# First tiles and PSUM banks of the SwiGLU and of the last part laid over other memory, and the first SwiGLU products in another order

## The chip, the cores and the metric

The program runs on one core of one Trainium2 chip. The metric is the device time of one execution in microseconds (us), as a median of several runs. PE is TensorE, DVE VectorE, ACT ScalarE, POOL GpSimd, and SP SyncE, which issues every DMA of this kernel. A named tile such as `wg` lies in SBUF or in PSUM; a name that ends in `_d` is a tensor in DRAM.

## The reference

One layer of a backbone with 2048 latent tokens of width 1024: gated linear attention (GLA, in both directions, with 256 context tokens ahead), its out projection, a residual, and a SwiGLU network of hidden width 2816 with another residual. Everything is float32.

```
h_lat = modulate(rms_norm(x, norm_g[0]), mod[0], mod[1])
o     = head_rms_norm(o_forward + flip(o_backward), gla_norm_g)
y_lat = (o * silu(r)) @ gla_w_out                          # out projection
lat   = x + mod[2] * rms_norm(y_lat, norm_g[1])
h     = modulate(rms_norm(lat, norm_g[2]), mod[3], mod[4])
gate, up = split(h @ ffn_w_in)                             # SwiGLU, first layer
out   = lat + mod[5] * rms_norm((silu(gate) * up) @ ffn_w_out, norm_g[3])
```

## The kernel before

Each float32 product is three matmuls on high and low parts. A matrix that comes from DRAM in float32 is therefore first cast to a rounded high part on ACT, and the low part, source minus high part, is formed on DVE.

The program has four stages, each with its own pools of tiles, taken as stacks on the left and the right side of SBUF and PSUM. A pool may lie over an earlier pool's memory, and its first write then waits for that memory's last readers.

- **Prologue, projections, attention**, up to about 828 us. The two scan states `Tf` and `Tb` come from the context tokens.
- **Out projection** (`p2`), 828 to 1078 us: for each block `gc` of 128 rows from 15 down to 0, steps `b0` (loads; the backward state `E` from `Tb` or from the block before), `b1` (products `o<-E,qb`, L695), `b2` (norm, transposes `tp` L722, gate), `b3` (products `py`, L86 to L88) and `b4` (norm, residual, store of `l1`, L754). After each four blocks `h2_units` makes transposed SwiGLU input: `first` (L769) writes two block matrices to `T_d`; `second` loads them back (`bl`, L775 and L776), and forms the sums and differences of Strassen's method (L781) and stores them (L778, L782).
- **SwiGLU, first layer** (`p3`), 1078.7 to 1944.6 us: 88 features of 7 products each, with the weight block as the stationary operand (`whl`, cast at L933, low part L934) and one of 7 tiles `T` as the moving one (L951). A product is 12 matmuls, 128x512. `load_T` (L860 to L862) loads a `T` tile in four DMAs of 256 KB, each with a cast and a subtraction. The order of products in the chain is P1, P2, P6, P7, P5, P4, P3; X collects P1, P6, P5 and P3, Y is P2, and Z collects P7 and P4. Row half 1 is worked first, then half 0; the `T` tiles of half 0 are loaded over those of half 1 as these fall free.
- **Last part** (`p4`), 1955 to 2383 us: products of the SwiGLU sums `ar` (loaded from `S_d`, `ring`, L1023 to L1028) with blocks of the second weight matrix `wr` (from `wraw`, `w2_block`, L1036 to L1038) in PSUM banks X and W (L1074), then norm, residual and the result.

A scheduler decides the order in which instructions stand in each engine's queue; the engines then work their queues in order. SP issues all DMAs in its order, so a DMA whose semaphore isn't there yet holds up all behind it. In addition each DMA shares one of eight semaphores with the DMA eight places ahead, and waits for that one.

At the end of the out projection, 4 units of `second` for half 1 of the SwiGLU input are still to be made (`pend`); the loads of the `T` tiles for P7, P5, P4 and P3 go into a pool `hR` on the right side, which opens only when these units' tiles are closed.

Of the kernel before, what the change touches and what calls it, by code (L numbers as in the profile page):

```python
# [34 lines left out]
def trunk(ctx, tc, x, cx, modw, cols, rows, consts, wqkr, wv, wvg, wgate, wout, w1, w2, out):  # L35
# [17 lines left out]
    qb_d = [dram.tile([128, H, 128], F32, name=f"qb_d{c}") for c in range(NC_)]  # L53

# [120 lines left out]
    Tf = gp.tile([128, H, DV], F32, name="Tf")  # L175
    glt = [c1.tile([128, 128], F32R, name=f"glt{i}") for i in range(4)]
# [177 lines left out]
    def gla_stages(g, i, c, first):  # L354
# [279 lines left out]
    p2t = ExitStack()  # L634
    sp = p2.enter_context(tc.tile_pool(name="sp", bufs=2, reuse_waits="tile"))
# [14 lines left out]
    def back(gc):  # L650
# [13 lines left out]
        def b0():  # L664
# [3 lines left out]
            qb = sp.tile([128, H, 128], F32, name="qb2", tag="qb2", bufs=3)  # L668
# [124 lines left out]

    order = list(range(NC_ - 1, -1, -1))
# [28 lines left out]
    for i, gc in enumerate(order):  # L823
# [27 lines left out]
    hR = p3.enter_context(tc.tile_pool(name="hR", bufs=1, reuse_waits="tile", side="right"))  # L851
    ps3z = p3.enter_context(tc.tile_pool(name="ps3z", bufs=1, space=PSUM, reuse_waits="tile", side="right"))
    T = {}

    def load_T(p, i):
        pool = hL if i in (P1, P2, P6) else hR
        t = pool.tile([128, 4, 2, GT], F32R, name=f"T{i}", tag=f"T{i}", bufs=1)
        for k in range(4):
            raw = t[:, k, 1, :].bitcast(F32)
            sync.dma_start(out=raw, in_=T_d[p][i][k])  # L860
            nc.scalar.copy(out=t[:, k, 0, :], in_=raw)  # L861
            nc.vector.tensor_sub(out=t[:, k, 1, :], in0=raw, in1=t[:, k, 0, :].bitcast(F32))  # L862
        T[i] = t
# [130 lines left out]
    feats = {}  # L994
    for i in CHAIN:
        load_T(1, i)
    n = len(seq)
    for t in range(n + 1):
        if t < n:
            feats[t] = Feat(*seq[t])  # L1000
        for lag, i in ((0, P1), (1, P5), (0, P2), (1, P4), (0, P6), (1, P3), (0, P7)):
            j = t - lag
            if not 0 <= j < n:
# [6 lines left out]
        if t >= 2 and t % 2 == 0:  # L1010
# [12 lines left out]
    def ring(tag, src):  # L1023
        t = r4.tile([128, 2, 512], F32R, name=tag, tag=tag, bufs=14)
# [6 lines left out]
    def w2_block(i, fp):  # L1031
# [158 lines left out]
```

## Time and profile before

| | |
|---|---|
| three runs | 2386.19, 2387.81, 2392.54 us, median 2387.81 |
| the profiled execution | 2384.77 us, of it a span of 2383.0 us in the trace |
| PE busy | 2302.0 us, 97% of the span |
| DVE, ACT, POOL busy | 1557.7, 1068.8 and 186.6 us |
| mean granted clock of PE | 0.986 of full speed |
| DMA | 463.98 MB, mean 195 GB/s |

All times below are microseconds from the start of the span. A queue name with q, such as SPq, stands for the sequencer of an engine. "[7.09 <-ACT whl L933]" behind a row says that the engine was idle for 7.09 us before it, and that the last event that it waited for was the ACT instruction of L933 that writes `whl`. PE matmuls overlap, so their durations sum to more than the time between their starts.

### The profile page before, as it was taken

How to read it: one execution, taken by the hardware profiler on the slowest of the kernel's cores; microseconds unless marked ns; L12 is line 12 of the kernel's file. 1: busy time of each engine (PE TensorE's matmuls, PEld its weight loads, DVE VectorE, ACT ScalarE, POOL GpSimd, SP SyncE). 2: the span in 40 equal slices, each digit the busy share in tenths (PEclk: the TensorE clock that was granted, in tenths of full speed). 3: DMA queues.
4: the chain of work that ended last, by engine and by line, in shares of the span. 5: the costliest groups of instructions: out<-in, count | busy, mean ns of one | idle time of the engine just before them, and what ended most of it. 6: DMA issues, size and time to landing. Idle time of an engine off the chain costs nothing.

```text
span 2383.0 us, 32426 instructions
## 1 busy us (share of the span) xinstructions
PE 2302.0 (97%) x11546; PEld 1939.9 (81%) x11546; DVE 1557.7 (65%) x2478; ACT 1068.8 (45%) x1947; POOL 186.6 (8%) x274
## 2 busy tenths in 40 slices
PE   8999999999998999897999999999999989999998
PEld 4898898898898878685888888888888868888887
DVE  6756666766658576658776666866666647466554
ACT  3535445445547544335433333533333336554552
POOL 1100000000001033631000000000000000001001
PEclk9999999999999999997999999999999999999999
DMA  8765468565455587758787332633233248559655
GB/s 299 225 208 173 148 197 285 177 210 208 153 191 191 206 274 257 243 186 309 258 264 259 125 111 93 230 102 115 97 106 107 75 149 284 191 192 330 201 181 177
DMA packets 228902, 463.98 MB, mean 195 GB/s; under 512 B 22530, under 2 KB 66178, under 8 KB 228740
## 3 DMA queue, kind: packets, MB, share of 16 engines
q1 hardware_dynamic: 228740, 461.92, 57.3%
q8 instruction: 90, 1.47, 0.3%
q14 instruction: 72, 0.59, 0.1%
HBM read 331.27 MB, written 130.56 MB: 194 GB/s over the span
## 4 chain that ended last, share of the span: by engine, by line
PE 52%; DMA 0%; DVE 0%; SPq 0%; ACT 0%; issue 0%; POOLq 0%; POOL 0%; ACTq 0%
PE X L951 20%; PE Z L951 10%; PE X L1074 10%; PE W L1074 8%; PE Y L951 5%; DMA wraw<-w 0%; DMA T<-T_d 0%; DMA T_d<-hf 0%; DVE sa L984 0%; DVE bl L781 0%; DVE y L1055 0%; SPq L906 0%; DVE t L781 0%; DVE hf L781 0%; DVE a L974 0%
## 5 line engine op out<-in xcount | busy, mean ns | idle before, releaser
L951 PE MATMUL X<-T,whl 128*128 128x512 f32 x2112 | 495.7, 390 | 8.2 <-ACT whl L933 7.1
L951 PEld LDWEIGHTS X<-T,whl 128*128 128x128 f32 x2112 | 396.6, 188 | 91.5 <-ACT whl L933 7.5
L951 PE MATMUL Z<-T,whl 128*128 128x512 f32 x1056 | 256.2, 391 | 9.1 <-ACT T L861 9.1
L1074 PE MATMUL X<-wr,ar 128*128 128x512 f32 x1056 | 242.3, 391 | 10.6 <-ACT wr L1038 10.6
L1074 PEld LDWEIGHTS X<-wr,ar 128*128 128x128 f32 x1056 | 199.2, 189 | 52.8 <-ACT wr L1038 11.1
L951 PEld LDWEIGHTS Z<-T,whl 128*128 128x128 f32 x1056 | 199.3, 189 | 51.6 <-ACT T L861 9.5
L86 PE MATMUL pj<-hhi,whi 128*128 128x512 f32 (+1 forms) x544 | 213.6, 395 | 2.1 <-DVE hhi L75 1.4
L87 PE MATMUL pj<-hlo,whi 128*128 128x512 f32 (+1 forms) x544 | 211.4, 389 | 0.0
L88 PE MATMUL pj<-hhi,wlo 128*128 128x512 f32 (+1 forms) x544 | 210.4, 387 | 0.0
L73 ACT CAST whi<-wf 128x1024 fp32r<-128x1024 f32 x104 | 109.0, 1048 | 192.7 <-PE pj L87 84.4
L1028 DVE TENSOR_TENSOR ar<-ar 128x512 fp32r<-128x512 f32 x154 | 106.2, 691 | 131.1 <-ACT ar L1027 130.6
L76 DVE TENSOR_TENSOR wlo<-wf,whi 128x1024 fp32r<-128x1024 f32 x104 | 126.8, 1220 | 86.5 <-ACT whi L73 81.0
L1074 PE MATMUL W<-wr,ar 128*128 128x512 f32 x792 | 180.5, 389 | 0.0
L1074 PEld LDWEIGHTS W<-wr,ar 128*128 128x128 f32 x792 | 148.7, 188 | 30.8
L1027 ACT CAST ar<-ar 128x512 fp32r<-128x512 f32 x154 | 95.5, 621 | 154.6 <-DMA ar<-S_d 107.0
L86 PE MATMUL pj<-whi,hhi 128*128 128x256 f32 x432 | 125.0, 289 | 6.3 <-DVE gs L292 4.9
L951 PE MATMUL Y<-T,whl 128*128 128x512 f32 x528 | 127.7, 390 | 0.0
L87 PE MATMUL pj<-wlo,hhi 128*128 128x256 f32 x432 | 123.2, 285 | 2.8 <-DVE wlo L76 2.8
L88 PE MATMUL pj<-whi,hlo 128*128 128x256 f32 x432 | 122.7, 284 | 0.0
L87 PEld LDWEIGHTS pj<-hlo,whi 128*128 128x128 f32 x544 | 103.5, 190 | 21.3 <-DVE hlo L76 2.2
L86 PEld LDWEIGHTS pj<-hhi,whi 128*128 128x128 f32 x544 | 103.1, 191 | 21.5 <-DVE hhi L75 1.6
L88 PEld LDWEIGHTS pj<-hhi,wlo 128*128 128x128 f32 x544 | 103.4, 190 | 19.7
(231 smaller groups left out, 4273.7 us busy)
## 6 DMA issues: line engine op xcount, KB each, us to landing
ar<-S_d SPq DMA_DIRECT2D x154, 256.0 KB, 3.0
wf<-wqkr SPq DMA_DIRECT2D x68, 512.0 KB, 3.9
wg<-w SPq DMA_DIRECT2D x44, 512.0 KB, 3.5
wu<-w SPq DMA_DIRECT2D x88, 256.0 KB, 2.7
S_d<-sa SPq DMA_DIRECT2D x88, 256.0 KB, 2.0
wr<-W_d SPq DMA_DIRECT2D x88, 256.0 KB, 3.0
wf<-wv SPq DMA_DIRECT2D x36, 512.0 KB, 3.8
wl<-w SPq DMA_DIRECT2D x66, 256.0 KB, 3.7
```

The lines of the kernel that those rows point to most:

```text
L73: nc.scalar.copy(out=hi, in_=src)
L76: nc.vector.tensor_sub(out=lo, in0=src, in1=hi.bitcast(F32))
L86: nc.tensor.matmul(out=ps, lhsT=ahi, rhs=bhi, start=start, stop=False)
L87: nc.tensor.matmul(out=ps, lhsT=ahi, rhs=blo, start=False, stop=False)
L88: nc.tensor.matmul(out=ps, lhsT=alo, rhs=bhi, start=False, stop=stop)
L951: nc.tensor.matmul(out=ps, lhsT=w[:, a, ks], rhs=t[:, k, b, :], start=first and k == 0 and n == 0, stop=k == 3 and n == 2, skip_group_chec ...
L1027: nc.scalar.copy(out=t[:, 0, :], in_=raw)
L1028: nc.vector.tensor_sub(out=t[:, 1, :], in0=raw, in1=t[:, 0, :].bitcast(F32))
L1074: nc.tensor.matmul(out=po[j], lhsT=a[:, x, 128 * j:128 * j + 128], rhs=w[:, z, :], start=first and fp == 0 and n == 0, stop=fp == NFP - 1 ...
```

## The change

In the attention part the state `Tb` loses its own pool, lies in that stage's pool, and is stored in DRAM (`Tb_d`, 512 KB); the out projection loads it back into a `ub2` buffer. The buffers of `qb2` go from 3 to 2. A new pool `hG` at the bottom of the out projection's left side holds the `T` tile of P1, which is loaded inside the out projection (`gc == 3`). The SwiGLU's weight pool `w3` comes ahead of `hL`, `hL` takes P2, P6 and P7, and `hR` P5, P4 and P3. The first products of two features are written out by hand. In the last part the ring of 14 `ar` and 14 `wr` tiles is cut into a first share (4 `ar` in `rA`, 10 `wr` and the 4 `wraw` in `rB`) and a rest (`rC`), and the X banks move to the right side of PSUM.

```diff
@@ attention part @@
-    tbp = pT.enter_context(tc.tile_pool(name="tbp", bufs=1))
-    Tb = tbp.tile([128, H, DV], F32, name="Tb")
+    Tb = gp.tile([128, H, DV], F32, name="Tb")
...
+                        st.dma_start(out=Tb_d, in_=Tb.rearrange("p h v -> p (h v)"))
@@ out projection @@
+    hG = p3.enter_context(tc.tile_pool(name="hG", bufs=1, reuse_waits="tile"))
-            qb = sp.tile([128, H, 128], F32, name="qb2", tag="qb2", bufs=3)
+            qb = sp.tile([128, H, 128], F32, name="qb2", tag="qb2", bufs=2)
             if gc == NC_ - 1:
+                Tb = sp.tile([128, H, DV], F32, name="ub2", tag="ub2", bufs=2)
+                sync.dma_start(out=Tb.rearrange("p h v -> p (h v)"), in_=Tb_d)
...
+        if gc == 3:
+            load_T(1, P1)
     p2.close()
@@ SwiGLU @@
+    w3 = p3.enter_context(tc.tile_pool(name="w3", bufs=2, reuse_waits="tile"))
     hL = p3.enter_context(tc.tile_pool(name="hL", bufs=1, reuse_waits="tile"))
-    w3 = p3.enter_context(tc.tile_pool(name="w3", bufs=2, reuse_waits="tile"))
...
-    for u in pend:
-        u()
-    p2t.close()
-    hR = ...
-        pool = hL if i in (P1, P2, P6) else hR
+    T_pool.update({i: hL for i in (P2, P6, P7)})
...
-    for i in CHAIN:
-        load_T(1, i)
+    feats = {0: Feat(*seq[0]), 1: Feat(*seq[1])}
+    load_T(1, P2)
+    for j, i in ((0, P1), (1, P1), (0, P2)):
+        feats[j].product(i)
+    load_T(1, P6)
+    feats[1].product(P2)
+    load_T(1, P7)
+    pend.pop(0)()
+    feats[0].product(P6)
+    for u in pend:
+        u()
+    p2t.close()
+    hR = p3.enter_context(tc.tile_pool(name="hR", bufs=1, reuse_waits="tile", side="right"))
+    ps3z = p3.enter_context(tc.tile_pool(name="ps3z", bufs=1, space=PSUM, reuse_waits="tile", side="right"))
+    T_pool.update({i: hR for i in (P3, P4, P5)})
+    for i in (P5, P4, P3):
         load_T(1, i)
+    for j, i in ((0, P7), (1, P6), (1, P7), (0, P5), (0, P4), (0, P3)):
+        feats[j].product(i)
-    for t in range(n + 1):
+    for t in range(2, n + 1):
@@ last part @@
-    r4 = p4.enter_context(tc.tile_pool(name="r4", bufs=1, reuse_waits="tile"))
+    rA = p4.enter_context(tc.tile_pool(name="rA", bufs=1, reuse_waits="tile"))
     y4 = p4.enter_context(tc.tile_pool(name="y4", bufs=1, reuse_waits="tile"))
+    rB = p4.enter_context(tc.tile_pool(name="rB", bufs=1, reuse_waits="tile"))
+    rC = p4.enter_context(tc.tile_pool(name="rC", bufs=1, reuse_waits="tile"))
...
+    def slot(tag):
+        i = count[tag] % 14
+        count[tag] += 1
+        first, nf = {"ar": (rA, 4), "wr": (rB, 10)}[tag]
+        pool, sfx, nb = (first, "", nf) if i < nf else (rC, "2", 14 - nf)
+        return pool.tile([128, 2, 512], F32R, name=tag, tag=tag + sfx, bufs=nb)
...
-        raw = r4.tile([128, 512], F32, name="wraw", tag="wraw", bufs=4)
+        raw = rB.tile([128, 512], F32, name="wraw", tag="wraw", bufs=4)
```

Four places show how the queues move. A row is the line of code, the operation, what it writes and reads, and the shape; line numbers behind the change are those of the changed code, a few higher or lower than before.

The first is SP's queue where the out projection starts (`ub2`, `qb2` and `op2` are the loads of `b0`, `wof` the weights of the out projection). Before:

```order
L667 DMA ub2_8324<-ub_d15_160 128x1024
L669 DMA qb2_8326<-qb_d15_176 128x512
L671 DMA op2_8328<-op_d15_144 128x1024
L645 DMA wof_8348<-wout 128x1024
L645 DMA wof_8352<-wout 128x1024
L659 DMA rt_8364<-r_d3_77 128x4x128
L246 DMA r_d3_77<-stg_8398 128x512
L667 DMA ub2_8423<-ub_d14_159 128x1024
L645 DMA wof_8356<-wout 128x1024
L645 DMA wof_8360<-wout 128x1024
```

And after:

```order
L669 DMA ub2_8326<-ub_d15_160 128x1024
L671 DMA qb2_8328<-qb_d15_176 128x512
L673 DMA op2_8330<-op_d15_144 128x1024
L679 DMA ub2_8332<-Tb_d_177 128x1024
L647 DMA wof_8352<-wout 128x1024
L647 DMA wof_8356<-wout 128x1024
L661 DMA rt_8368<-r_d3_77 128x4x128
L245 DMA r_d3_77<-stg_8402 128x512
L669 DMA ub2_8427<-ub_d14_159 128x1024
L647 DMA wof_8360<-wout 128x1024
L647 DMA wof_8364<-wout 128x1024
```

The load of `Tb` stands behind block 15's three loads, ahead of the weights; the load of block 14's `ub2` now takes the buffer that the state lay in, and so waits for the ACT operation that forms block 15's `E`. On PE the first `o` products of block 15 stand 17 matmuls (`pj`) further back in the queue than before.

The second is SP's queue at the end of the out projection (`l1_d1` and `l1_d0` are the last residual stores, `T0`, `T1`, `T5`, `T6`, `T4` the tiles of P1, P2, P6, P7 and P5, `wg` and `wu` the first weights of the SwiGLU, `bl` the loads of a unit of `second`). Before:

```order
L860 DMA T5_10965<-T_d15_90 128x512 x3
L754 DMA l1_d1_114<-y2_10622 128x1024
L775 DMA bl_10823<-T_d00_78 128x512
L776 DMA bl_10823<-T_d01_79 128x512
L860 DMA T5_10965<-T_d15_90 128x512
L903 DMA wg_11030<-w1 128x1024
L906 DMA wu0_11032<-w1 128x512
L906 DMA wu1_11033<-w1 128x512
L870 DMA wl_11113<-w2 128x512
L754 DMA l1_d0_113<-y2_10732 128x1024
L775 DMA bl_10850<-T_d00_78 128x512
L776 DMA bl_10850<-T_d01_79 128x512
```

And after, first the weights:

```order
L758 DMA l1_d1_114<-y2_10639 128x1024
L903 DMA wg_10839<-w1 128x1024
L906 DMA wu0_10841<-w1 128x512
L906 DMA wu1_10842<-w1 128x512
L903 DMA wg_10845<-w1 128x1024
L906 DMA wu0_10847<-w1 128x512
L906 DMA wu1_10848<-w1 128x512
L804 DMA T1_10851<-T_d11_86 128x512
```

then what follows them:

```order
L758 DMA l1_d0_113<-y2_10749 128x1024
L804 DMA T1_10851<-T_d11_86 128x512 x3
L804 DMA T5_10918<-T_d15_90 128x512 x4
L804 DMA T6_10949<-T_d16_91 128x512 x4
L779 DMA bl_10962<-T_d00_78 128x512
L780 DMA bl_10962<-T_d01_79 128x512
L782 DMA T_d02_80<-hf2_10972 128x512
L779 DMA bl_11012<-T_d00_78 128x512
L780 DMA bl_11012<-T_d01_79 128x512
```

The weights of two features now come straight behind the store `l1_d1` and ahead of all other `T` tiles, and the `bl` loads of the first unit, which stood right behind `l1_d1` before, come behind eleven `T` loads that follow `l1_d0`.

The third is PE's queue at the same place, from the last product of the out projection on (X, Y and Z are the PSUM tiles; the numbers of the `T` tiles, before: 10939 P1, 10952 P2, 10965 P6, 10978 P7, 10991 P5; after: 10485 P1, 10851 P2, 10918 P6, 10949 P7, 11101 P5). Before:

```order
L951 MATMUL X<-T_10939,whl 128x512 x3
L951 MATMUL Y<-T_10952,whl 128x512 x4
L102 MATMUL tp<-ident,xh 128x128 x4
L951 MATMUL Y<-T_10952,whl 128x512 x6
L951 MATMUL X<-T_10965,whl 128x512 x12
L951 MATMUL X<-T_10939,whl 128x512 x12
L951 MATMUL Y<-T_10952,whl 128x512 x12
L951 MATMUL Z<-T_10978,whl 128x512 x12
L951 MATMUL X<-T_10991,whl 128x512 x12
```

And after:

```order
L951 MATMUL X<-T_10918,whl 128x512 x3
L100 MATMUL tp<-ident,xh 128x128 x5
L951 MATMUL Y<-T_10851,whl 128x512 x12
L951 MATMUL X<-T_10918,whl 128x512 x8
L100 MATMUL tp<-ident,xh 128x128 x8
L951 MATMUL X<-T_10918,whl 128x512 x12
L951 MATMUL Z<-T_10949,whl 128x512 x24
L951 MATMUL X<-T_11101,whl 128x512 x12
```

Ahead of the piece of before stands the beginning of the first feature's P1 and P2; the piece's first P7 product (Z) stands behind five products (P1 and P2 of both features, P6 of the first). Ahead of the piece of after stand the P1 of both features (24 matmuls) and the P2 of the first; the two P7 products stand behind six products, and the first P5 product, the last row, behind eight.

The fourth is SP's queue at the start of the last part (`sa` and `a` are the last sums of the SwiGLU, `A5` a vector for the last norm). Before:

```order
L979 DMA S_d03_95<-a1_17496 128x512
L979 DMA S_d04_96<-sa_17558 128x512
L979 DMA S_d05_97<-sa_17561 128x512
L979 DMA S_d02_94<-sa_17564 128x512
L1021 DMA A5_17582<-A_d1_190 128x1024
L1026 DMA ar_17604<-S_d10_99 128x512
L1036 DMA wraw_17608<-w2 128x512
L1026 DMA ar_17625<-S_d10_99 128x512
L1036 DMA wraw_17629<-w2 128x512
L1026 DMA ar_17646<-S_d10_99 128x512
```

And after:

```order
L1056 DMA ar_17638<-S_d10_99 128x512
L1056 DMA ar_17659<-S_d10_99 128x512
L1056 DMA ar_17680<-S_d10_99 128x512
L979 DMA S_d00_92<-a0_17311 128x512
L979 DMA S_d06_98<-sa_17558 128x512
L979 DMA S_d01_93<-a0_17463 128x512
L1051 DMA A5_17595<-A_d1_191 128x1024
L979 DMA S_d03_95<-a1_17499 128x512
L979 DMA S_d04_96<-sa_17561 128x512
L979 DMA S_d05_97<-sa_17564 128x512
L979 DMA S_d02_94<-sa_17567 128x512
L1066 DMA wraw_17621<-w2 128x512
```

Three of the four early `ar` loads are in the piece (the fourth stands one row ahead of it); they and `A5` now stand ahead of the last stores, while the first `wraw` still follows the last store of `sa`.

## Rows read from the trace of the kernel before

**Rows 1.** The list of who waited for whom, for PE over the whole span: engine, tile and line that waited, what it waited for, us in total, times, the longest.

```profile
PE X L1074 <- ACT wr L1038: 10.6, 1, 10.6
PE Z L951 <- ACT T L861: 9.1, 1, 9.1
PE X L951 <- ACT whl L933: 7.1, 1, 7.1
...
PE tp L722 <- DVE on L703: 5.6, 4, 2.5
```

**Rows 2.** Stretches of the span: length, busy time of each engine with its count, granted clock of PE as a share of full speed, DMA share, GB/s.

```profile
820.00:830.00 10.00, 8.46 (x39) 6.38 (x38) 7.44 (x14) 6.51 (x11) 1.76 (x2) 1.00 0.76 259
...
920.00:940.00 20.00, 20.00 (x104) 16.79 (x103) 13.33 (x31) 8.42 (x24) 6.04 (x8) 1.00 0.92 301
...
1100.00:1150.00 50.00, 40.92 (x171) 32.90 (x170) 41.97 (x69) 24.37 (x44) 0.00 (x0) 0.90 0.90 313
...
1111.00:1131.00 20.00, 13.14 (x48) 10.23 (x49) 15.07 (x25) 10.87 (x20) 0.00 (x0) 0.74 1.00 360
```

**Rows 3.** The timeline of SP's queue around the start of the SwiGLU: start, duration of the issue, what.

```profile
1077.59 0.32 SPq L754 DMA_DIRECT2D l_d<-y  x1
1077.95 0.43 SPq L775 DMA_DIRECT2D bl<-T_d  x1
...
1079.80 0.43 SPq L903 DMA_DIRECT2D wg<-w  x1
...
1087.13 0.33 SPq L754 DMA_DIRECT2D l_d<-y  x1
...
1110.86 0.32 SPq L782 DMA_DIRECT2D T_d<-bl  x1
```

**Rows 4.** Timelines of ACT, DVE and PE in the same stretch, in this order.

```profile
1085.09 1.14 ACT L933 CAST whl<-wg 128x512 fp32r<-128x512 f32 x2 [0.98 <-DMA wg<-w]
...
1106.58 1.45 ACT L103 ACTIVATE hf<-tp,mcol 128x512 f32<-128x512 f32 x2
...
1085.88 1.22 DVE L753 TENSOR_TENSOR y<-y,xt 128x1024 f32<-128x1024 f32 x1
...
1093.06 0.69 DVE L781 TENSOR_TENSOR bl<-hf,bl 128x512 f32<-128x512 f32 x1
...
1110.14 0.69 DVE L781 TENSOR_TENSOR bl<-bl,t 128x512 f32<-128x512 f32 x1
...
1078.29 0.39 PE L88 MATMUL py<-wo_hi,olo 128*128 128x512 f32 x1
1085.76 1.22 PE L951 MATMUL X<-T,whl 128*128 128x512 f32 x2 [7.09 <-ACT whl L933]
```

**Rows 5.** The chain that ended last, through the same stretch: start, us, what.

```profile
1113.01 4.16 DMA T<-T_d
...
1117.19 0.63 ACT T L861
...
1117.86 5.21 PE Z L951 x12
...
1134.03 2.72 PE Z L951 x12
```

**Rows 6.** The chain that ended last at the start of the last part, and the second hundred and thirty-two matmuls of that part.

```profile
1947.43 0.70 DVE sa L984
...
1948.15 0.32 SPq L979
...
1949.56 4.98 DMA wraw<-w
...
1954.56 0.63 ACT wr L1038
...
1955.23 31.92 PE X L1074 x132
...
1987.15 29.92 PE W L1074 x132
```

**Rows 7.** Median time from issue to landing of loads, over the whole program: out<-in, count, KB each, us.

```profile
wu<-w SPq DMA_DIRECT2D x88, 256.0 KB, 2.7
...
wr<-W_d SPq DMA_DIRECT2D x88, 256.0 KB, 3.0
...
ub<-ub_d SPq DMA_DIRECT2D x15, 512.0 KB, 5.5
...
qb<-qb_d SPq DMA_DIRECT2D x16, 256.0 KB, 5.7
```

**Rows 8.** Timelines of SP, ACT and PE at the start of the out projection, in this order.

```profile
813.36 0.32 SPq L671 DMA_DIRECT2D op<-op_d  x1
...
815.75 0.78 SPq L667 DMA_DIRECT2D ub<-ub_d  x1
...
809.74 1.71 ACT L678 ACTIVATE E<-Tb,fb 128x256 f32<-128x256 f32 x4
...
817.24 1.89 PE L695 MATMUL o<-E,qb 128*128 128x256 f32 x8
...
829.58 1.99 PE L695 MATMUL o<-E,qb 128*128 128x256 f32 x8 [0.79 <-DMA qb<-qb_d]
...
831.77 0.48 PE L86 MATMUL py<-wo_hi,ohi 128*128 128x512 f32 x1
```

More of the change, by code (lines that the diff above doesn't have):

```diff
@@ L53, in trunk @@
     qb_d = [dram.tile([128, H, 128], F32, name=f"qb_d{c}") for c in range(NC_)]
+    Tb_d = dram.tile([128, D], F32, name="Tb_d")
     ident = cst.tile([128, 128], F32, name="ident")
@@ L792, in h2_units, with load_T @@
         return [lambda k=k: second(k) for k in range(4)]
+    T, T_pool = {}, {P1: hG}
+    def load_T(p, i):
+        t = T_pool[i].tile([128, 4, 2, GT], F32R, name=f"T{i}", tag=f"T{i}", bufs=1)
+        for k in range(4):
+            raw = t[:, k, 1, :].bitcast(F32)
+            sync.dma_start(out=raw, in_=T_d[p][i][k])
+            nc.scalar.copy(out=t[:, k, 0, :], in_=raw)
+            nc.vector.tensor_sub(out=t[:, k, 1, :], in0=raw, in1=t[:, k, 0, :].bitcast(F32))
+        T[i] = t
     order = list(range(NC_ - 1, -1, -1))
@@ L993, in trunk @@
     seq = [(p, f) for p in (1, 0) for fp in range(NFP) for f in (fp, fp + NFP)]
-    feats = {}
-    for i in CHAIN:
-        load_T(1, i)
-    n = len(seq)
-    for t in range(n + 1):
+    n = len(seq)
+    feats = {0: Feat(*seq[0]), 1: Feat(*seq[1])}
[14 more added lines that the diff above has]
+    for i in (P5, P4, P3):
+        load_T(1, i)
+    for j, i in ((0, P7), (1, P6), (1, P7), (0, P5), (0, P4), (0, P3)):
+        feats[j].product(i)
+    for _ in range(2):
+        units.pop(0)()
+    for t in range(2, n + 1):
         if t < n:
@@ L1002, in trunk @@
             j = t - lag
-            if not 0 <= j < n:
+            if not j < n:
                 continue
@@ L1009, in trunk @@
             units.pop(0)()
-        if t >= 2 and t % 2 == 0:
+        if t % 2 == 0:
             feats[t - 1].combine(feats[t - 2])
@@ L1016, in trunk @@
     p4 = ExitStack()
-    r4 = p4.enter_context(tc.tile_pool(name="r4", bufs=1, reuse_waits="tile"))
+    rA = p4.enter_context(tc.tile_pool(name="rA", bufs=1, reuse_waits="tile"))
     y4 = p4.enter_context(tc.tile_pool(name="y4", bufs=1, reuse_waits="tile"))
-    ps4 = p4.enter_context(tc.tile_pool(name="ps4", bufs=1, space=PSUM, reuse_waits="tile"))
+    rB = p4.enter_context(tc.tile_pool(name="rB", bufs=1, reuse_waits="tile"))
+    rC = p4.enter_context(tc.tile_pool(name="rC", bufs=1, reuse_waits="tile"))
+    ps4 = {"W": p4.enter_context(tc.tile_pool(name="ps4", bufs=1, space=PSUM, reuse_waits="tile")),
+           "X": p4.enter_context(tc.tile_pool(name="ps4x", bufs=1, space=PSUM, reuse_waits="tile", side="right"))}
+    count = {"ar": 0, "wr": 0}
+    def slot(tag):
[4 more added lines that the diff above has]
+        return pool.tile([128, 2, 512], F32R, name=tag, tag=tag + sfx, bufs=nb)
     A5 = y4.tile([128, D], F32, name="A5")
@@ L1023, in ring @@
     def ring(tag, src):
-        t = r4.tile([128, 2, 512], F32R, name=tag, tag=tag, bufs=14)
+        t = slot(tag)
         raw = t[:, 1, :].bitcast(F32)
@@ L1059, in out_group @@
         lo, hi = slice(0, 512), slice(512, 1024)
-        X = [ps4.tile([128, 512], F32, name="X4", tag=tx, bufs=4) for j in range(4)]
+        X = [ps4[tx].tile([128, 512], F32, name="X4", tag=tx, bufs=4) for j in range(4)]
         y0 = [y4.tile([128, D], F32, name="y0", tag="y0", bufs=6) for j in range(4)]
@@ L1067, in out_group @@
             if i in (P2, P7):
-                W = [ps4.tile([128, 512], F32, name="W4", tag=tw, bufs=4) for j in range(4)]
+                W = [ps4[tw].tile([128, 512], F32, name="W4", tag=tw, bufs=4) for j in range(4)]
             po = W if i in (P2, P7, P4) else X
```

17 lines of the change are left out of this document (2 added, 15 removed).

## The prediction

> **What bounds the kernel now.** The page's first part comes first: PE is busy for 2302.0 of 2383.0 us, so all its idle time is 81 us, 3.4% of the span, and no edit that leaves the matmuls as they are can bring more than that and the slower clock that follows a gap. The list of who waits for whom then says where PE's idle time lies [rows 1]. Its three longest single waits, 10.6, 9.1 and 7.1 us, stand at just the two seams that the change touches: the last product with `wr` and `ar` (start of the last part), the first Z and the first X product (start of the SwiGLU). Together they are 26.8 us. The waits of `tp` for `on` (5.6 us in four) belong to the out projection's start. Between the seams PE runs without a gap, in 920 to 940 us for 20.00 of 20 us [rows 2]. So I read three places, each by the chain or the timelines: which wait ends last there, and what is next when it goes. The changed order tells who stands behind whom, the trace of before how long each takes.
>
> A gap also costs afterwards. Twelve matmuls of a product take 2.72 us at full clock; the first twelve after the 9.08 us gap took 5.21 us [rows 5], and the granted clock of the stretch 1111 to 1131 us is 0.74, that is partly the lower level of 1.2 GHz and partly 2.4 GHz [rows 2]. In the last part the first 132 matmuls took 31.92 us, the next 132 29.92 us [rows 6]. So a gap that vanishes altogether gives back about 2.0 to 2.5 us beside itself; one that only shrinks need not.
>
> **Start of the SwiGLU.** Before: the out projection's last matmul starts at 1078.29; PE waits 7.09 us until ACT has cast `wg` (1085.09) and starts X at 1085.76 [rows 4]. The `wg` load went out at 1079.80 [rows 3] and was 5.3 us on its way (to the cast at 1085.09); ahead of it stood the store of `l1_d1` (1077.59), two `bl` loads and a `T` load [rows 3]. In the changed queue `wg` comes straight behind that same store, which waits for POOL's residual sum. So it goes out at 1077.59 + 0.37 = 1077.96, 1.8 us earlier, and with less ahead of it should land about 4.5 to 5 us later, at 1082.5 to 1083.0. With cast and subtraction 0.7 us X starts near 1083.4, 2.3 us earlier. The laying over of free memory alone would allow much more, but SP's order doesn't let it.
>
> Those 2.3 us are no gain of their own, because a second gap follows that decides. Before, PE had done five products when it stood still for 9.08 us until the `T` tile of P7 was there: the last unit's subtraction on DVE at 1110.14, its store at 1110.86 [rows 3, 4], the `T` load at 1113.01 landing after 4.16 us, cast 0.63, Z at 1117.86 [rows 5]. That tile now lies where it need not wait for the units. The first tile that does is P5's, and by then eight products stand ahead on PE, not five: 3 x 2.72 = 8.16 us of work done earlier [rows 5]. Against it stands how much later P5's tile comes. The units' first DVE operation starts at 1093.06 and the last at 1110.14 + 0.69, 17.8 us for four units, paced by loads, transposes and evictions [rows 4]. In the changed queue the first unit's `bl` loads, out at 1077.95 before [rows 3], stand behind `l1_d0` and eleven `T` loads. `l1_d0` went out at 1087.13, after DVE's sum of 1085.88 + 1.22 [rows 3, 4]; it comes some 2 us earlier, near 1085.3, as DVE has less ahead. Eleven loads of 0.26 MB are 2.9 MB, at the 360 GB/s of the busiest stretch [rows 2] 8.0 us; with the 2 us or so of a store's or a load's way the eleventh lands near 1095.5 and the two `bl` 1.5 us later, near 1097.5. So the units start near 1098 in place of 1093.06, 4.9 us later, end near 1115.8, and P5's product starts near 1122.8 instead of Z at 1117.86. Gain: 8.16 - 4.9 = **3 us**. PE isn't short of time for the eight products: the two P7 products wait for the last evictions of the units (before at 1106.58 + 1.45 [rows 4], now near 1113), take 5.4 us and end near 1118.5; a wait of about 4 us stays ahead of P5, and some 5 us ahead of Z, beside 5 us ahead of X. The gaps remain in another cut, and so does the clock's price.
>
> The bounds: if the `bl` loads land as early as before (they compete for bandwidth only, not in order), the units end at 1110.83 and the whole 8.2 us is kept. If the units, whose DVE operations now share the queue with the subtractions of eight more `T` parts (0.69 each, 5.5 us by a row of the same shape and engine [rows 4]), start and end 9 us later, the gain is -1. I take 3, since the load order is fixed and the subtractions mostly fall before the `bl` land.
>
> The Trainium skill, page "DMA: Bandwidth & Descriptors", section "Queues, rings and completion order", says that each DMA engine takes the descriptors of one queue's ring in order. By that rule, which speaks against this change, the eleven prefetched tiles must pass before the `bl` data move, as in the sum above; the opposite would give the 8.2 us. The loads' landing times here, 2.7 us in the median and 5.3 us for `wg` behind other loads [rows 3, 4, 7], agree with it.
>
> **Start of the last part.** Before: the last DVE operation on `sa` (1947.43 + 0.70), its store at 1948.15, then A5, `ar` and at 1949.56 the first `wraw`, which took 4.98 us to land because 0.75 MB went ahead; cast at 1954.56, PE at 1955.23 [rows 6]. After: A5 and four `ar` are loaded earlier and `ar` is already cast, but the first `wraw` still stands behind the last store of `sa`, which needs the same DVE operation. So it goes out at 1948.15 + 0.37 = 1948.5, with nothing large ahead, lands after 2.7 to 3.0 us (the medians for 256 KB [rows 7]) at about 1951.4, and with 0.67 us for the cast PE starts near 1952.1. Gain: **3 us** of the 10.6. Free banks and free tiles can't show, since the data come last. Bounds: 2 if it lands no faster than 4 us; 12.6 (10.6 and 2.0 of clock) if the gap vanished altogether.
>
> The same page, section "Anatomy of one DMA — SWDGE (gpsimd) path", gives a DMA 2.0 us and its bytes at 436 GB/s; an estimate by it is 2.6 us for 256 KB, and the gain would be 3.3 us. No load of before shows that alone at this place.
>
> **Start of the out projection.** This part pays. `Tb` was in SBUF: ACT formed block 15's `E` at 809.74, and PE's `o` products followed at 817.24 [rows 8]. Now its load goes out after `op2` (813.36 + 0.37 = 813.73 [rows 8]); 512 KB of this kind take 5.5 us in the median [rows 7], so 819.2; `E` 1.71 us, and `o` starts near 821.1, 3.9 us later. Behind it wait block 15's norm, its transposes and the first `py` (831.77 [rows 8]). Until then PE still has `pj` work to fill in, which runs out near 828.8; PE had idle time there already (8.46 of 10 us busy [rows 2]), so part of the delay is taken by slack. Block 14's `ub2` load, at 815.75 before, waits for `E` until 820.9, but it is needed only for the E after. I put the first `py` 2.5 us later and half a microsecond won back in block 14's waits (0.79 before its `o` [rows 8], 5.6 in all ahead of `tp` [rows 1]): **-2 us**, between 0 (all in slack) and -3.9 (none).
>
> **Edits at nothing.** The store of `Tb_d` lies in the context part, with no reader for hundreds of microseconds. The `T` tile of P1 is loaded near 920 to 940 us, 1 MB at a DMA share of 0.92 while PE is full [rows 2]; its casts and subtractions are 4 x 0.63 and 4 x 0.69 on engines that aren't full (DVE 13.33, ACT 8.42 of 20 us). If `qb2` with two buffers or that load came late, a block's `o` would wait (rival 3); I put 0, at worst -2. The PSUM banks and the ring's pools change no order on PE beyond the seams.
>
> **Sum.** 2384.77 - 3 - 3 + 2 = 2380.8 us for an execution like the profiled one. The median of three is 3.0 us above that one, so 2383.8 us against 2387.81, 0.17% faster. A difference under 0.3% (7.2 us) can't be told from none here.
>
> **Rivals.**
> 1. *The `bl` loads aren't held up* (0.17). The units end at 1110.83; 8.2 + 3 - 2 = 9.4 us: 2378.4. For it: the landing of 360 GB/s leaves room if the `T` loads are issued slowly; against it: their place in the queue.
> 2. *The seams close as they are laid out* (0.12): eight products reach P5 without a gap, and the last part starts without one. 8.2 + 4 + 2.5 at the SwiGLU and 12.6 in the last part, less 2: 25 us, 2362. Decided by whether the units end before 1108 and `wraw` goes out before 1944. Against it: both stand behind operations that I can name. The Trainium skill's rule to issue a DMA early and wait for it late (same page, "Rules for kernel authors") would give this where nothing holds the issue up.
> 3. *Slower* (0.09): `qb2` with two buffers. A block's `qb2` load may then go out only when `o` of the block two ahead is done, and takes 5.7 us in the median [rows 7]. If `o` had to wait for it, each of some 14 blocks would pay. Sixteen blocks from the first `py` at 831.77 to the last at 1078.29 are 15.4 us a block [rows 4, 8]; the load fits in as long as `o` is done a block ahead, as PE's 20.00 of 20 us at 920 to 940 suggests [rows 2]. At 1 us a block it is 14 - 4 = 10 us slower, 2398; from 0.8 us a block it passes the bound of 0.3%.
> 4. *Nothing moves* (0.10): losses and gains cancel, 2387.8 within 2 us.
> The forecast has 0.52.
>
> Faster by over 0.3%: rivals 1 and 2 nearly whole, a little of the forecast, 0.31. Slower: most of rival 3, 0.07. The range holds the forecast with its bounds and rivals 1 and 4, and leaves out rival 2 and the far part of 3: 2373 to 2391; the likeliest case alone 2380 to 2388.
>
> **What would show it.** PE's wait ahead of the first X near 5 us, released by the cast of `wg`; waits ahead of Z and P5 that sum to about 9 us, with eight products done before P5; the `bl` loads issued after 1089 and landed near 1097; in the last part a wait near 7.5 us released by the cast of `wr`, with `wraw` issued right behind the last `sa` store; `o` of block 15 near 821 and the first `py` near 834. The prediction is wrong if the `bl` loads land near 1090, if the wait ahead of the last part is under 4 us, or if the first `py` moves by under 1 or over 5 us.

## The result, and the profile after

The changed kernel takes 2403.11 us (median of four runs, 2399.15 to 2404.54) against 2389.38 of the kernel before beside it: a ratio of 1.0055 with an interval of 1.004 to 1.007, some 13 us slower. I had forecast 0.17% faster, with slower by over 0.3% at 0.07. The profiled execution took 2402.34 us, of it a span of 2400.6 us, 17.6 more than before: the profiled execution of before, 2384.77 us, lies 4.6 us under its median, so differences to its trace come out too large by some us in all.

Where these lie is read from PE's starts and ends in each trace, cut at four places: 796 us (until there both kernels do the same on PE), the last `py` of the out projection, the last matmul of the SwiGLU, the first and the last matmul of the last part. The table gives the difference to the trace of before, in us, one execution each; the kernels E1 to E10 are those of the experiments below.

| | until 796 | out projection | SwiGLU | wait ahead of the last part | last part |
|---|---|---|---|---|---|
| after | +2.2 | +9.0 | +4.2 | -2.9 | +5.0 |
| E1 | -0.4 | +11.6 | +2.0 | -3.0 | +1.2 |
| E2 | +5.6 | 0.0 | +0.5 | +0.1 | +4.3 |
| E3 | -1.0 | +9.6 | +1.9 | -3.0 | +4.8 |
| E4 | +2.9 | +1.7 | +1.5 | +0.2 | +0.4 |
| E5 | -0.3 | +1.9 | +5.0 | -3.0 | +1.4 |
| E6 | +1.5 | +4.6 | +1.3 | -2.9 | +0.4 |
| E7 | +1.6 | +0.1 | +1.3 | -1.2 | +1.0 |
| E8 | -0.1 | +0.3 | +0.4 | -9.4 | +2.7 |
| E9 | +3.4 | +2.6 | +0.8 | -10.8 | -0.6 |
| E10 | 0.0 | +3.6 | +1.5 | -0.8 | +1.3 |

E2, E7, E8 and E9 leave the code of the first three columns as it was before. Their differences there, -0.1 to 5.6, 0 to 2.6 and 0.4 to 1.3, are what one execution differs from another by; a difference within that is not read from a single trace.

PE's part of the page's list of engines, after (before: 2302.0 us, 97%):

```profile
PE 2313.4 (96%) x11546; PEld 1941.5 (81%) x11546; DVE 1557.9 (65%) x2478; ACT 1069.5 (45%) x1947; POOL 183.4 (8%) x274
```

PE is busy for 11.4 us longer with as many matmuls: part of the loss is slower work, no wait. Who waited for whom on PE, after (us in total, times, the longest), which answers [rows 1]:

```profile
PE X L951 <- ACT T L805: 10.2, 1, 10.2
...
PE X L1104 <- ACT wr L1068: 7.7, 1, 7.7
...
PE tp L726 <- DVE on L707: 5.9, 4, 2.5
...
PE X L951 <- ACT whl L933: 5.3, 2, 4.2
...
PE Z L951 <- ACT hf L101: 1.4, 1, 1.4
```

The three long waits (ahead of the first X, of the first product that needs the units, and of the last part) became 4.2, 10.2 and 7.7: 22.1 in place of 26.8 us. The three waits are a little shorter, and the kernel is slower. So the loss is mostly in places that the prediction put at nothing.

**Out projection.** Four stretches of 10 us, columns as in [rows 2]; before, PE was busy for 20.00 of 20 us in the first two:

```profile
920.00:930.00 10.00, 10.00 (x52) 8.46 (x51) 6.92 (x14) 0.59 (x1) 1.93 (x1) 1.00 0.94 333
930.00:940.00 10.00, 9.39 (x46) 7.55 (x45) 6.41 (x13) 6.31 (x17) 4.84 (x6) 1.00 0.68 213
940.00:950.00 10.00, 9.62 (x46) 7.59 (x44) 5.27 (x12) 3.52 (x11) 1.43 (x3) 1.00 0.85 281
950.00:960.00 10.00, 7.57 (x24) 5.46 (x25) 7.53 (x14) 5.50 (x13) 5.95 (x8) 0.66 0.32 105
```

ACT (the fourth busy column) works 0.59 of 10 us in the first. In the last, PE does 24 matmuls instead of about 50, at a granted clock of 0.66. The issue of the early `T` tile's loads on SP, and the timelines of ACT and PE:

```profile
923.88 1.63 SPq L804 DMA_DIRECT2D T<-T_d  x3
...
929.41 1.31 ACT L805 CAST T<-T 128x512 fp32r<-128x512 f32 x2 [9.47 <-DMA T<-T_d]
930.62 0.41 ACT L704 ACTIVATE on<-op 128x256 f32<-128x256 f32 x1
...
946.27 0.62 ACT L805 CAST T<-T 128x512 fp32r<-128x512 f32 x1 [9.90 <-DMA T<-T_d]
946.79 0.41 ACT L704 ACTIVATE on<-op 128x256 f32<-128x256 f32 x1
...
950.43 1.15 PE L726 MATMUL tp<-ident,on 128*128 128x128 f32 x8 [0.81 <-DVE on L707]
952.57 1.57 PE L699 MATMUL o<-E,qb 128*128 128x256 f32 x4 [0.99 <-ACT hf L101]
955.15 2.07 PE L699 MATMUL o<-E,qb 128*128 128x256 f32 x4 [1.01 <-ACT hf L101]
```

ACT stands for 9.47 and 9.90 us at casts of the early `T` tile, whose data aren't there yet; at the first it had stood for 4 us when SP issued the load. The block's norm (`on`, L704) is queued right behind the cast, and behind `on` come the transposes, the gate and the `py`.

**Start of the SwiGLU.** SP's queue, DVE and PE, after (the rows of before are [rows 3, 4]):

```profile
1088.36 0.32 SPq L758 DMA_DIRECT2D l_d<-y  x1
1088.73 0.42 SPq L903 DMA_DIRECT2D wg<-w  x1
...
1095.82 0.33 SPq L758 DMA_DIRECT2D l_d<-y  x1
1096.20 7.29 SPq L804 DMA_DIRECT2D T<-T_d  x11
1103.84 0.32 SPq L779 DMA_DIRECT2D bl<-T_d  x1
...
1130.48 0.60 SPq L786 DMA_DIRECT2D T_d<-bl  x1
...
1133.40 2.70 SPq L804 DMA_DIRECT2D T<-T_d  x6
...
1111.78 0.69 DVE L957 TENSOR_TENSOR g<-g,Y 128x512 f32<-128x512 f32 x1 [0.21 <-PE Y L951]
...
1113.59 0.69 DVE L785 TENSOR_TENSOR bl<-hf,bl 128x512 f32<-128x512 f32 x1
...
1093.98 8.49 PE L951 MATMUL X<-T,whl 128*128 128x512 f32 x24 [4.15 <-ACT whl L933]
...
1123.31 5.75 PE L951 MATMUL Z<-T,whl 128*128 128x512 f32 x24 [1.36 <-ACT hf L101]
...
1139.22 5.51 PE L951 MATMUL X<-T,whl 128*128 128x512 f32 x12 [10.16 <-ACT T L805]
```

The queue is as forecast (`wg` behind `l1_d1`, `bl` behind `l1_d0` and eleven `T` loads), and eight products stand before P5. But the units' first DVE operation comes 9.7 us after the first `bl` was issued. The two `bl` loads of the first unit, issued at 1103.84 and 1104.53, took this long to land:

```profile
DMA to landing us min/median/max: 5.3/5.3/5.4
```

So the data were there at 1109.9, and DVE took them up 3.7 us later.

**Last part.** The chain at its start, after (before: [rows 6]):

```profile
1963.53 0.32 SPq L979
...
1963.96 3.01 DMA wraw<-w
...
1966.99 0.63 ACT wr L1068
...
1967.66 33.41 PE X L1104 x132
2001.07 30.27 PE W L1104 x132
```

The wait is what I had forecast. But 132 matmuls without any gap now take 30.27 us, not 29.92, and the twelve groups behind it 30.03 to 30.27 us each.

### The profile page after: what moved, and what is told of

It is laid out like the page before. It is cut to its first block, busy times and chain, and to the rows that moved or that the text cites. A ratio compares the mean times of both kernels' runs of the same rounds, so it can differ in the third digit from the quotient of the medians.

```text
span 2400.6 us, 32416 instructions
## 1 busy us (share of the span) xinstructions
PE 2313.4 (96%) x11546; PEld 1941.5 (81%) x11546; DVE 1557.9 (65%) x2478; ACT 1069.5 (45%) x1947; POOL 183.4 (8%) x274
## 4 chain that ended last, share of the span: by engine, by line
PE 52%; DMA 1%; DVE 1%; ACT 0%; issue 0%; SPq 0%; POOL 0%; POOLq 0%; ACTq 0%; DVEq 0%
PE X L951 20%; PE X L1104 10%; PE Z L951 10%; PE W L1104 8%; PE Y L951 5%; DMA T<-T_d 0%; DMA wg<-w 0%; DMA wl<-w 0%; DMA bl<-T_d 0%; DVE bl L785 0%; DMA wraw<-w 0%; DMA T_d<-bl 0%; DMA T_d<-hf 0%; ACT T L805 0%; POOL y L757 0%
## 5 line engine op out<-in xcount | busy, mean ns | idle before, releaser
L951 PE MATMUL X<-T,whl 128*128 128x512 f32 x2112 | 501.3, 393 | 15.5 <-ACT T L805 10.2
L951 PEld LDWEIGHTS X<-T,whl 128*128 128x128 f32 x2112 | 400.3, 190 | 101.7 <-ACT T L805 10.8
L1104 PE MATMUL X<-wr,ar 128*128 128x512 f32 x1056 | 245.8, 394 | 7.7 <-ACT wr L1068 7.7
L1104 PEld LDWEIGHTS X<-wr,ar 128*128 128x128 f32 x1056 | 200.1, 190 | 52.4 <-ACT wr L1068 8.1
L1104 PE MATMUL W<-wr,ar 128*128 128x512 f32 x792 | 182.0, 391 | 0.0
L1104 PEld LDWEIGHTS W<-wr,ar 128*128 128x128 f32 x792 | 148.7, 188 | 32.3
```

The lines of the kernel that those rows point to most:

```text
L951: nc.tensor.matmul(out=ps, lhsT=w[:, a, ks], rhs=t[:, k, b, :], start=first and k == 0 and n == 0, stop=k == 3 and n == 2, skip_group_chec ...
L1104: nc.tensor.matmul(out=po[j], lhsT=a[:, x, 128 * j:128 * j + 128], rhs=w[:, z, :], start=first and fp == 0 and n == 0, stop=fp == NFP - 1 ...
```

## The experiments

**Theory**: three causes, (a) the casts of the early `T` tile that hold up ACT, (b) the units that start late, (c) where the ring's tiles lie in SBUF. For (c) I worked out, from the starts of single matmuls in the traces and the tiles' addresses in the programs, the time from one matmul to the next; `ar` is the stationary and `wr` the moving operand of L1104. **Rivals**: the reload of `Tb` or `qb2` with two buffers costs the out projection's time (the prediction's rival 3); PE is slower since other tiles or PSUM banks are used, whatever the address.

| last part | start of `ar`, of `wr`, modulo 256 bytes | ns per matmul |
|---|---|---|
| before, all places | 224, 224 | 226.7 |
| after, ring places 0 to 3 of 14 | 224, 160 | 233.3 |
| after, place 4, then 5 to 13 | 160, 160 | 229.2, then 226.7 |
| E1, all places | 224, 224 | 226.7 |
| E2, all places | 224, 32 | 228.9 |

At place 4 the first six matmuls still take 228 to 236 ns, although both tiles start at 160 there; why is not shown.

**E1, after, with the ring moved by 64 bytes** (a spare tile in `y4`):

```diff
     A5 = y4.tile([128, D], F32, name="A5")
+    pad = y4.tile([128, 16], F32, name="pad")
+    nc.gpsimd.memset(pad, 0.0)
```

> The changed kernel with one spare tile of 64 bytes a partition in the pool ahead of rB, so that all ar and all wr tiles of the last part's ring start at the same place modulo 128 bytes (96). In the changed kernel the first four ar tiles start at 96 and all wr tiles at 32. Theory: a matmul whose stationary and moving tiles differ in that place takes 233.3 ns instead of 226.7, here 4 of 14 ring places; with the spare tile every 132 matmuls of the last part take 29.9 us as in the kernel before, not 30.0 to 30.3, and the time falls by some 3.8 us to about 2399. Rival: the new PSUM banks of X, or the greater distance of the tiles, make them slow: 132 still take 30.0 to 30.3 us and the time stays near 2403.

Measured: 2397.26 us, ratio 1.0034 (1.0021 to 1.0047). Its chain, for the first and second 132 matmuls of the last part:

```profile
1965.51 33.09 PE X L1106 x132
1998.60 29.92 PE W L1106 x132
```

All further groups of 132 are at 29.92 to 29.93. In the last part the trace gives back 3.8 us; the whole kernel gives back 5 us by the ratios, whose intervals overlap a little. What is left of the last part's loss, 1.2 us, is in its first 132 matmuls, behind the wait: 33.09 us for 31.92 before. The rival of other banks and tiles falls: they are the same as after.

**E2, before, with `wr` moved by 64 bytes** against `ar`:

```diff
+        if not padded:
+            padded.append(r4.tile([128, 16], F32, name="pad"))
+            nc.gpsimd.memset(padded[0], 0.0)
         t = r4.tile([128, 2, 512], F32R, name="wr", tag="wr", bufs=14)
```

> The kernel before with one spare tile of 64 bytes a partition between the ar and the wr tiles of the last part, so that all 14 wr tiles start at 32 modulo 128 bytes and all ar tiles at 96. Theory: all 1848 matmuls of the last part take 233.3 ns instead of 226.7: 132 take 30.8 us instead of 29.92, and the time rises by 12.2 us, 0.5%. Rival (banks or distance): 29.92 us, no change.

Measured: 2397.13 us, ratio 1.0035 (1.0022 to 1.0047). The same row of E2's chain:

```profile
1993.85 30.21 PE W L1078 x132
```

The kernel before becomes slower by an offset alone: +4.3 us in its last part. The ratio says 5 to 11 us; the rest lies, in this trace, in the 5.6 us until 796, where the code is as before, and is not explained. The size I missed: 228.9 ns, not 233.3. Here `wr` lies 64 bytes on from `ar` modulo 256, after it lay 64 bytes back; that the sign makes the difference is a guess.

**E3, after, with the `T` tile of P1 loaded behind the loop:**

```diff
-        if gc == 3:
-            load_T(1, P1)
     p2.close()
...
+    load_T(1, P1)
     load_T(1, P2)
```

> The changed kernel, with the T tile of P1 loaded after the out projection's code, together with that of P2, instead of inside it. Theory: inside, its casts stand on ACT ahead of the norm of a block and wait 9.5 us for the loads, twice; without it the out projection wins back about 7 us. The tile is needed by the first product, so up to 2 us may be given back ahead of X. About 2397. Rival: the reload of Tb and the two qb2 buffers are what makes the out projection longer: no gain there, 2403 or later.

Measured: 2401.55 us, ratio 1.0051 (1.0032 to 1.0069), out projection +9.6. The edit tested nothing: the scheduler pulled loads and casts to the same place in the queues, and ACT stood at the first cast for 9.35 us (a row of ACT's timeline):

```profile
927.46 1.28 ACT L805 CAST T<-T 128x512 fp32r<-128x512 f32 x2 [9.35 <-DMA T<-T_d]
```

**E4, before, with the reload of `Tb` and two `qb2` buffers alone** (the diff's first five pieces):

```diff
+                        st.dma_start(out=Tb_d, in_=Tb.rearrange("p h v -> p (h v)"))
-            qb = sp.tile([128, H, 128], F32, name="qb2", tag="qb2", bufs=3)
+            qb = sp.tile([128, H, 128], F32, name="qb2", tag="qb2", bufs=2)
+                Tb = sp.tile([128, H, DV], F32, name="ub2", tag="ub2", bufs=2)
+                sync.dma_start(out=Tb.rearrange("p h v -> p (h v)"), in_=Tb_d)
```

> The kernel before with only Tb through DRAM and two qb2 buffers. Theory: block 15's first o comes 3 to 4 us later and the out projection 1 to 2 us, nothing else moves: 1.5 us slower. Rival: the two qb2 buffers cost each block some time, the out projection is 7 us longer or more.

Measured: 2392.79 us, ratio 1.0017 (1.0007 to 1.0026), 2 to 6 us. PE, at the start of the out projection:

```profile
835.20 3.78 PE L697 MATMUL o<-E,qb 128*128 128x256 f32 x8 [2.05 <-DMA qb<-qb_d]
...
839.41 0.47 PE L84 MATMUL py<-wo_hi,ohi 128*128 128x512 f32 x1
```

One `o` waits 2.05 us for `qb2`. A loss of 1 us in each block would be 14 us or so; the out projection took 1.7 us longer, within what executions differ by. Rival 3 falls. How the 2 to 6 us split between the reload and the two buffers is not shown.

**E5, E1 with the casts held back**: casts and subtractions of the early tile are placed on ACT and DVE behind the norm that makes the SwiGLU input of block 3; ACT works on them at 1070.54 instead of 929.72 us.

```diff
+        anchor["act"] = nc.scalar.activation(out=junk, in_=src, func=AF.Square, accum_out=ss).ins
+        anchor["dve"] = nc.vector.tensor_scalar_mul(out=junk, in0=src, scalar1=rs[:, 0:1]).ins
...
         if gc == 3:
-            load_T(1, P1)
+            with tc.issue_after(anchor["act"]), tc.issue_after(anchor["dve"]):
+                load_T(1, P1)
```

> e1 with the four casts and four subtractions of the P1 tile queued behind the norm of block 3 on ACT and DVE (some 90 us later); its loads stay where they are on SP. Theory: what costs the out projection time is ACT standing 9.5 us at the first cast of the tile, with a block's norm behind it; so some 7 us come back, about 2390. Rival: the loads themselves, with SP standing ahead of them until the stores have landed and 1 MB more on a busy queue: no gain, about 2397.

Measured: 2394.19 us, ratio 1.0013 (1.0001 to 1.0025), 0.21% (5 us, for 7 expected) under E1's ratio. Stretches of E5:

```profile
940.00:950.00 10.00, 10.00 (x52) 8.40 (x50) 5.03 (x9) 6.32 (x13) 4.67 (x8) 1.00 0.44 149
950.00:960.00 10.00, 10.00 (x48) 8.22 (x47) 8.18 (x18) 4.40 (x13) 3.64 (x8) 1.00 0.72 229
```

The hole at 950 to 960 us is gone, and of the out projection's 11.6 us in E1 9.7 are back: (a) is shown. The same four loads still go out in this stretch (921 to 934 us, 924 to 941 in E1); so it was neither the bandwidth nor the load but the wait of the casts. At the SwiGLU's start 3.0 us of it are lost again (+5.0 instead of +2.0): the first X waits for its weight and again for its low part, Z for 3.4 us, P5 for 8.38 us.

**E6, E5 with two of the units written ahead of the `T` tiles of P2 and P6:**

```diff
     feats = {0: Feat(*seq[0]), 1: Feat(*seq[1])}
+    pend.pop(0)()
+    pend.pop(0)()
     load_T(1, P2)
...
     load_T(1, P7)
-    pend.pop(0)()
     feats[0].product(P6)
```

> e5 with the first two units of second written ahead of the T tiles of P2, P6 and P7 and of the first products, so that their bl loads stand ahead of eleven T loads on SP. Theory: the queue order delays the units; they start 6 us or more earlier, the wait ahead of P5 falls from 8 to 10 us to 5 or less, 4 to 5 us faster than e5. Rival: DVE, which is busy 9.8 of 10 us at 1110 to 1120, paces the units: the wait moves to other places and the time stays that of e5.

Measured: 2390.31 us, ratio 0.9999 (0.999 to 1.0008): level with before, 3 to 4 us under E5 for 4 to 5 expected. SP and PE of E6:

```profile
1091.82 0.33 SPq L760 DMA_DIRECT2D l_d<-y  x1
1092.19 0.43 SPq L909 DMA_DIRECT2D wu<-w  x1
1092.66 0.79 SPq L781 DMA_DIRECT2D bl<-T_d  x1
...
1110.39 0.80 PE L954 MATMUL Y<-T,whl 128*128 128x512 f32 x1 [3.84 <-ACT T L807]
...
1133.63 5.26 PE L954 MATMUL X<-T,whl 128*128 128x512 f32 x13 [5.38 <-ACT whl L936]
```

`bl` now goes out 0.84 us after `l1_d0` instead of eight. PE's wait behind the two P7 products falls from 8.38 to 5.38 (two matmuls of the third feature now stand ahead of P5, and their weight's cast ends it), while Y waits for its `T` tile, which comes later: the SwiGLU's column goes from +5.0 to +1.3. So (b) is shown for E5, where the held casts had made the start worse. In the changed kernel itself the column is +4.2, and +2.0 and +1.9 in E1 and E3, against up to 1.3 where the code is as before: there (b) is worth some 1 to 4 us, and no run takes it away alone.

**E7, before, with the last part of the change alone**, its ring aligned as in E1, and the residual's loads behind the ring's:

```diff
+        with tc.issue_after(ring_last[0]):
+            sync.dma_start(out=l1, in_=l1_d[gc])
```

> The kernel before with the last part of the change alone, all ring tiles at the same place modulo 128, and the loads of l1 queued behind the ring's loads. Theory: the wait ahead of the last part is 7.7 us instead of 10.6, 132 matmuls take 29.92 us, and the time is 3 us shorter than before. Rival: something else of the changed last part costs time, and it isn't shorter.

Measured: 2388.06 us, ratio 0.9985 (0.9975 to 0.9994), 1 to 6 us faster. The wait became 9.4 us, not 7.7: four `wraw` and an `ar` go out at once, and the first takes longer to land than after's 3.01 us (a row of E7's chain).

```profile
1951.50 4.73 DMA wraw<-w
```

**E8, E7 with the four `wraw` over memory that falls free early:**

```diff
-        raw = rB.tile([128, 512], F32, name="wraw", tag="wraw", bufs=4)
+        raw = rA.tile([128, 512], F32, name="wraw", tag="wraw", bufs=4)
```

> e7 with the four wraw buffers in rA, behind the four ar, over the P1 and P2 tiles of the SwiGLU, which are free early; their loads then stand ahead of the last stores of sa on SP. Theory: the wait ahead of the last part falls to about 1.5 us (the last SiLU and the first cast of wr on ACT), the slower clock behind it goes too: 7 us from the wait and 1 to 2 us from the clock, 8 to 9 us faster than e7, 11 us faster than before (2378). Rival: the four ring places run out before the next ones are loaded, and the wait comes back after them: half the gain.

Measured: 2380.68 us, ratio 0.9956 (0.9941 to 0.9971), 10.5 us faster than before for 11 expected. PE of E8:

```profile
1946.33 0.49 PE L1090 MATMUL X<-wr,ar 128*128 128x512 f32 x1 [1.19 <-ACT wr L1053]
1949.33 25.92 PE L1090 MATMUL X<-wr,ar 128*128 128x512 f32 x106 [2.50 <-DVE wr L1054]
```

The data are there. Now the first `wr` holds PE up, whose low part DVE forms only behind the last sums (`sa`) of the SwiGLU.

**E9, E8 with the first four `wr` there too:**

```diff
-        first, nf = {"ar": (rA, 4), "wr": (rB, 10)}[tag]
-        pool, sfx, nb = (first, "", nf) if i < nf else (rC, "2", 14 - nf)
+        if i < 4:
+            pool, sfx, nb = rA, "", 4
+        elif tag == "wr" and i < 10:
+            pool, sfx, nb = rB, "1", 6
+        else:
+            pool, sfx, nb = rC, "2", 10 if tag == "ar" else 4
```

> e8 with the first four wr tiles also in rA, over the P1, P2 and P6 tiles of the SwiGLU, in place of memory that the last sums a and sa still use. Theory: in e8 PE still waited 1.2 us for the first cast and 2.5 us for a subtraction that stood behind the last sums on DVE; now casts and subtractions stand ahead of those, PE goes from the SwiGLU into the last part without a wait, and the clock stays: 4 to 5 us faster than e8, 2376. Rival: the fifth ring place comes too late (two loads of later tiles stand ahead of it on SP) and PE waits some 3 us there: as e8.

Measured: 2373.96 us, ratio 0.9943 (0.993 to 0.9957), some 14 us faster than before, 27 faster than after and 3 faster than E8 by the ratios. The trace is of one of the two longest of six executions, 2380.10 us. PE of E9:

```profile
1948.48 2.88 PE L951 MATMUL X<-T,whl 128*128 128x512 f32 x12
1951.20 11.04 PE L1094 MATMUL X<-wr,ar 128*128 128x512 f32 x48
1962.90 7.34 PE L1094 MATMUL X<-wr,ar 128*128 128x512 f32 x30 [0.65 <-ACT ar L1046]
```

PE goes from the last SwiGLU product straight into the last part, and the granted clock of 1940 to 1990 us is 1.00.

**E10, E6 with the last part of E9** (both diffs together):

> e6 (the change with equal places modulo 128, held casts, units first) with the last part of e9. Theory: what is left of the change beside its last part costs the 3 us that e6 and e4 show, so it ends 3 to 5 us behind e9, at 2380. Rival: its SwiGLU start and the last part help each other and it is the faster one.

Measured: 2392.03 us, ratio 1.0015 (1.0005 to 1.0026): no better than before, and 12 us over what I expected. SP of E10, PE's longest wait, and DVE's last reading of `wg`:

```profile
1953.62 0.76 SPq L1067 DMA_DIRECT2D ar<-S_d  x1
1954.43 0.63 SPq L1077 DMA_DIRECT2D wraw<-w  x1
...
PE X L1116 <- ACT wr L1079: 9.8, 1, 9.8
...
1916.29 0.69 DVE L939 TENSOR_TENSOR s<-wg,s 128x512 f32<-128x512 f32 x1
```

The wait is back, since the first `ar` and `wraw` again go out behind the last stores of `sa`. Why SP's queue has them there is not shown. By the programs' addresses, behind the P1 tile (19168 to 35552) lie in the layout of before the tiles of P2 and P6, which fall free early; in the changed layout it is the weight pool `w3` (35552 to 88800), used to the end, and I had not looked at this. But the four `wraw` lie over `wg` alone (35552 to 43744), which nothing reads after 1917 us, and the first `ar` over the P1 tile: in this trace neither waits for its memory. Of the ring's first pool only the last `wr` lies over memory (`whl`) that PE reads to the end. That the scheduler holds back the whole pool for it is a guess.

## Why the prediction was wrong, point by point

- **Edits at nothing: the step that failed first.** I priced the early `T` tile at 0, at worst -2, from the busy sums of ACT and DVE and the bandwidth: "engines that aren't full". The runs show a wait in its place: holding its casts back gave back 9.7 us in the out projection (E1 to E5), 5 us in the whole kernel by the ratio, since 3.0 us of it went again at the SwiGLU's start. A busy sum doesn't see a wait: I costed the casts' durations, but not what is queued behind a cast that waits for its load. The row was in the order of the changed kernel, `on` right behind the `T` cast.
- **Start of the SwiGLU, +3 in the sum: mis-sized, and of the wrong sign.** After the change three traces with the same code here (after, E1, E3) give -4.2, -2.0 and -1.9, where the unchanged code gives -0.4 to -1.3 (E2, E7 to E9). The wait ahead of X (4.15 for 5), `l1_d0` (1095.82, that is 1084.66 by the clock of before, shifted by the 11.16 us of the last `py`, for 1085.3), the landing of the first `bl` pair (1098.7 by that clock, for 1097.5) and the eight products were right. Wrong was the start of the units: 1113.59, that is 1102.4 by the same shift, for 1098. When the data are there, DVE is at `T` subtractions and at a `g` that waits for PE's Y; I had set this bound (9 us later, "the gain is -1") aside because "the subtractions mostly fall before the `bl` land". The units began 9.3 us later than before. Behind them, P5's product came another 2.1 us later after the units' end than in the sum, and the units themselves took 1.2 us less. So P5 starts at 1128.06 by the clock of before, 10.2 us after Z did, and 8.16 - 10.2 gives -2.0 in place of +3. The rest of after's 4.2 is within the 2.3 us by which the three traces differ.
- **The queue rule.** I had the loads move in the order of the queue, by the Trainium skill's rule that each DMA engine takes a ring's descriptors in order (page "DMA: Bandwidth & Descriptors", section "Queues, rings and completion order"). The trace agrees: the `bl` pair landed last, and near the forecast time. But 8.0 us of the way, from `l1_d0` to the issue of `bl`, stood on SP, where the eleven loads go out in 7.29 us: among them it waits 1.5 us, and ahead of the first `bl` 0.3 us, for the landing of `T` loads that went out before.
- **Last part, +3: right for the wait.** 7.7 us for 7.5, `wraw` behind the last `sa` store, landed after 3.01 us. (The prediction's estimate of 2.6 us by the Trainium skill, page "DMA: Bandwidth & Descriptors", section "Anatomy of one DMA — SWDGE (gpsimd) path", is for DMAs that another engine issues; the 3.01 decides.) Of the 2.9 us won, 1.2 were lost again in the first 132 matmuls behind the wait (E1).
- **The ring's pools at nothing: the tiles' offset.** I set them at nothing since they "change no order on PE beyond the seams". They move the tiles' addresses, and that cost about 5 us by E1's ratio, 3.8 by the trace. The diff shows new pools but not their addresses.
- **Reload of `Tb`, -2: about right**, 2 to 6 us by E4, which also has the two `qb2` buffers. `o` started at 823.29, 3.9 us late beside the 2.2 us until 796, as forecast. The first `py` did not come 2.5 but 3.8 us late beside these 2.2, so the slack took nearly nothing there; most of it was won back later in the stage (E4: +1.7 in all).

```profile
837.76 0.48 PE L84 MATMUL py<-wo_hi,ohi 128*128 128x512 f32 x1
```

- **Rivals.** The slower one named the wrong mechanism. Rival 1's sum is 9.2, not 9.4. Rival 2's price for the last seam, 12.6 us, was close (E9: 14 by the ratio, 11.4 by the last two columns), but the change doesn't reach it: that would have needed early places for `wraw` and `wr`, not only for `ar`. The signs of being wrong all watched the seams and the start of the out projection; none came up (the `py` beside the 2.2 us), while the loss arose elsewhere.

The steps from after to E6, by the ratios, are 5 us for the offset, 5 for the casts and 3 to 4 for the units. They follow one another, so it is no proof of each size that they add up to the 13 us: what it shows is that with all three E6 is level with before. What E6 keeps of the change, the reload of `Tb` and the shorter wait of the last part, nearly cancels. Each part is known to 2 us at best.

## What to carry to other kernels

A load moved early brings its consumer along: look in the queue of the engine that casts or copies it for what stands right behind, and price as a stall there the whole time until the load has landed, the time until it is issued included. (The Trainium skill, page "DMA: Bandwidth & Descriptors", section "Rules for kernel authors", says to wait late; here the issue was early and the wait was early too.) At a seam follow each buffer of the first products, raw data and converted tile alike, to the memory under it and to who frees that last; one buffer that is left can keep most of the wait. And look at where a new layout puts the operands: a change that moves no instruction can still change a matmul's time.

## What the runs showed of the hardware that I had not expected

The time of a 128x512 matmul on rounded float32 depended on where the two operands start: 226.7 ns with the same start modulo 256 bytes (but for the six matmuls at place 4), 228.9 and 233.3 where they differed by 64 bytes one way and the other. Two experiments that move nothing but this offset turn it on and off; why is not shown, and other offsets weren't tried.
